# One encoder layer with a mixture of experts: first transfers, filler matmuls, norm rows and preloads rearranged

## The chip, the cores and the metric

The kernel runs on one core of one Trainium2 chip. The metric is the time of one execution on the device in microseconds; a kernel's time is the median of several executions, and lower is better. A core has TensorE (PE in the profile, its weight loads PEld), VectorE (DVE), ScalarE (ACT), GpSimd (POOL) and SyncE (SP); SP only issues transfers here, and all large loads go through its one queue. Transfers between the chip's memory (HBM) and the on-chip memory are carried out by 16 DMA engines. Matmul results land in PSUM, in banks of 128 x 512 floats.

## What is computed

One layer over 512 tokens of width 1024, in float32: three token mixers side by side (neighbourhood attention, grouped-query attention, attention into 256 memory tokens), gated and projected, a layer norm, and then a mixture of 16 experts of which each picks 64 tokens, with a second layer norm. Cut to its frame:

```python
mkv = jnp.einsum('bmd,df->bmf', mem, w_mem_kv[l])      # memory keys and values, the first work
...
merged = jnp.sum(gates * proj, axis=2)
mix = jnp.einsum('bsd,de->bse', merged, w_out[l])
x = layer_norm(DN_ALPHA * x + mix, ln1_g[l], ln1_b[l])
ffn = expert_choice_ffn(x, w_router[l], w_gate_up[l], w_down[l])
x = layer_norm(DN_ALPHA * x + ffn, ln2_g[l], ln2_b[l])

def expert_choice_ffn(x, w_router, w_gate_up, w_down):
    aff = softmax(x @ w_router)                        # 512 x 16
    gate, idx = top_k(aff per expert, 64)              # each expert picks 64 tokens
    h = x[idx] @ w_gate_up                             # 16 x 64 x 2048
    ye = (silu(hg) * hu) @ w_down                      # 16 x 64 x 1024
    return zeros.at[idx].add(ye * gate)
```

The expert weights are 16 x (8 MB + 4 MB), 192 MB of some 250 MB that the kernel moves.

## The kernel before

**Order.** The program is written with a manual schedule: each engine runs its instructions in the order in which the Python code issues them, and waits only for data and for buffers. Buffers come from pools by tag; a tag with two or three buffers is taken in turns, and a new tile in a buffer waits until the old one has been read. PSUM has the tags `mm` (3 banks), `S` (2), `T` (2) and `Y` (1), line 60.

**The start (lines 182 to 209, `g_mem`).** Dense products before the experts are done in two pieces for precision: `hi_lo` (line 84) makes a rounded copy of an operand on ScalarE (L85) and the remainder on VectorE (L86), and three matmuls are summed, hi x hi, hi x lo and lo x hi (`t_piece`, lines 244 to 249). The weights before the experts come as 74 units of 512 KB; `Stream` loads and splits them a little ahead. The first work needs the transposed memory rows `memr` (1 MB) and unit 0, so both are loaded in three pieces each, in turns (L197 memory, L198 unit), of 2, 2 and 4 of the 8 slices k of the contraction. Behind them on SP stand units 1 to 5, then the four quarters of x in turns with units 6 to 9. `k_item(h)` makes the memory keys of head h from unit h: 24 matmuls of 256 columns.

**The middle.** Attention, gates and branch projections run with TensorE as the busiest engine. At the end of it the output projection (`wo_part`, lines 992 to 999; `w_rest`, line 1018) is done in parts per 128-token tile m, with the layer norm's statistics, router logits and top-64 search of earlier tiles between its parts.

**The routing stretch (lines 1047 to 1118).** After the last part of tile 3, TensorE transposes pieces of x (`r_transpose`), forms logits (`r_logits`), transposes affinities (`r_back`); VectorE does the row scale, the softmax (`affinity`) and the rounds of the top-64 search (`rounds`); ScalarE and GpSimd write the normed rows as two half-precision pieces (`x1_norm`, lines 983 to 988). `keep_warm(n)` issues n filler matmuls, identity by identity, whose result in a bank `warm2` is never read. `thp` broadcasts the cut per expert, `cnp` counts positions.

**The experts.** `Ring` (line 731) streams the expert weights in 192 pieces of 1 MB through 22 buffers, most of which belong to earlier stages and come free as these end: the order is the list `RING`; the last are `Ma` and `Mb` (x and its norm), and `VS` (a triangle for `cnp`). `ring.done` issues the next load when a piece has been used. The order is gate and up 0 to 3 of an expert, the four down pieces of the one before, gate and up 4 to 7; at the end the eight pieces of expert 15, the down pieces of expert 14, then those of 15, which are cut by quarters of the output columns. Per expert e: `gate_up` (L1184), `act_h`, and in the next expert's loop `h_transpose` and `down` (L1217). Side work is stepped between: `gather` of the next four experts' tokens (in the loop of e = 3, 7, 11), `residual`, and `combine`, which adds a pair of experts' results into `ACC` (4 token tiles of 1024 columns).

**The last expert and the tail.** In the loop of e = 15 stand, between its two halves, `ln_row` (eight small matmuls that broadcast the second norm's gain to all partitions, copied to `g2` by ScalarE) and `rows_of_norm` (eight matmuls that make six rows `gb` of gain and bias for a low-rank product). Then `last_down` does expert 15's down product by quarters q of 256 columns: `product(q)` (L1333, and its split into hi and lo on ScalarE and VectorE), for q = 0, 1 `add(q)` (scatter into a bank, sum into `ACC` on VectorE, statistics, multiplication by the gain on GpSimd), for q = 2, 3 `preload(q)` (L1325: `ACC` copied into PSUM by an identity matmul) and `add_in_psum(q)` (scatter on top of it), then statistics from PSUM. After the statistics of all quarters: mean and scale per row, transposed to rows, `times_g_psum` for q = 2, 3, and `low_rank` and `diag` matmuls that finish the norm before the stores.

Of the kernel before, what the change touches and what calls it, by code (L numbers as in the profile page):

```python
# [18 lines left out]
P = 128  # L19
D = 1024  # L20
# [21 lines left out]
def layer_kernel(ctx: ExitStack, tc: tile.TileContext, xt, xn, memt, wu, bgate, rpb, gains, wrt,  # L42
# [139 lines left out]
    memh = R("A3", [P, KD, 256], "memh", F32R)  # L182
    meml = R("A4", [P, KD, 256], "meml", F32R)
    memr = R("A2", [P, KD, 256], "memr")
    raw0 = twin("raw")
    hi0 = hi_tile(0)
    lo0 = lo_tile(0)
# [21 lines left out]
    ws.hl[0] = (hi0, lo0)  # L209
# [55 lines left out]

    ST = {}

    def g_mem():
# [7 lines left out]
        def k_item(h):  # L276
# [3 lines left out]
            t_unit(acc[:, :256], u, memh, meml)  # L280
# [766 lines left out]
    warm2 = PB("T", "warm2")  # L1047

    def keep_warm(n):
        for _ in range(n):  # L1050
            nc.tensor.matmul(warm2[:, :P], ident, ident, start=True, stop=True)
# [38 lines left out]
    keep_warm(26)  # L1090
# [13 lines left out]
    nc.tensor.matmul(thp[:, :NEXP], ones_f[:NEXP], dg, start=True, stop=True)  # L1104
    msk = cp.tile([P, NT, 2, NEXP], F16, name="msk")
# [10 lines left out]
    keep_warm(3)  # L1116
# [81 lines left out]
    def h_transpose(e):  # L1198
        h = HT[e]
        tp = PB("mm", f"ht{e}", (P, 4, P))  # L1200
# [90 lines left out]
    def rows_of_norm():  # L1291
# [17 lines left out]
    def last_down(g2):  # L1309
# [8 lines left out]
        cols = [slice(q * 256, q * 256 + 256) for q in range(4)]  # L1318
        for mp in range(2):
            acc_of(2 * mp)  # L1320
        xq = {(q, mp): PB("ST"[mp], f"xq{q}{mp}", (P, 2, 256)) for q in (2, 3) for mp in range(2)}

        def preload(q):
            for mp in range(2):
                nc.tensor.matmul(xq[q, mp], ident, ACC[mp][:, :, cols[q]], start=True, stop=False)  # L1325
# [45 lines left out]
        def stats(q, m):  # L1371
            nc.vector.bn_stats(st[:, m, q], xq[q, m // 2][:, m % 2])
# [264 lines left out]
```

## Time and profile before

| | us |
|---|---|
| median of 3 runs (lowest, highest) | 989.99 (987.61, 991.37) |
| the profiled execution's own time | 987.18 |
| its span | 985.4 |
| TensorE busy | 957.7 (97%) |
| VectorE busy | 452.0 (46%) |
| ScalarE busy | 269.6 (27%) |
| GpSimd busy | 75.0 (8%) |

The DMA engines moved 251.59 MB, 255 GB/s over the span, and 425 to 427 GB/s in the slices of the expert stage. The mean granted clock of TensorE was 0.991 of full speed. The profile shows one execution; times in it are microseconds from the span's start unless marked ns. A timeline row gives start, duration, engine, line, operation, output and inputs, shapes, and in brackets how long the engine had been idle and what ended that. A row of a stretch ("windows") gives its length, then the busy time and the number of instructions of PE, PEld, DVE, ACT and POOL, the granted clock, the busy share of the DMA engines and GB/s. A row of SyncE's waits gives who waited for what, the sum, the number of times and the longest. A matmul of two float32 operands shows as two rows.

### The profile page before, as it was taken

To read this page: it belongs to the slowest core of one execution; us is meant where nothing else is said; L and a number is where in the kernel's file an instruction comes from. 1 tells how busy PE (TensorE), PEld (TensorE's weight loads), DVE (VectorE), ACT (ScalarE), POOL (GpSimd) and SP (SyncE) were. 2 spreads that over 40 slices of the span, in tenths; PEclk is the share of its full clock that TensorE was granted. 3 is DMA by queue.
4 is the path that set the end of the run, shared out by engine and by line. 5 is a ranking of instruction groups with operands and counts; after the bars stand their busy time and mean duration, and the time that the engine had idled before them with its cause. 6 is when DMAs were issued, how large, how long until landed. Compare 5 with 4: busy or idle time off the path is not lost.

```text
span 985.4 us, 13380 instructions
## 1 busy us (share of the span) xinstructions
PE 957.7 (97%) x5412; PEld 624.7 (63%) x5412; DVE 452.0 (46%) x855; ACT 269.6 (27%) x532; POOL 75.0 (8%) x82
## 2 busy tenths in 40 slices
PE   8999999999999999999999999999999999997998
PEld 7999877889888888887886334433343333432445
DVE  5437768665276566236463155331332223230327
ACT  4434344454354454323232010100010001100121
POOL 0002303000032231000021000000000000000002
PEclk8999999999999999999999999999999999999999
DMA  8322111111343322575729999999999999999982
GB/s 342 101 71 81 60 48 65 63 46 44 91 123 109 102 81 77 219 280 187 263 104 410 401 426 426 425 427 425 427 425 425 427 427 427 426 427 426 427 368 86
DMA packets 52605, 251.59 MB, mean 255 GB/s; under 512 B 14112, under 2 KB 14784, under 8 KB 28992
## 3 DMA queue, kind: packets, MB, share of 16 engines
q1 hardware_dynamic: 51968, 249.44, 63.2%
q10 hardware_dynamic: 576, 1.31, 0.3%
q8 instruction: 42, 0.69, 0.3%
q14 instruction: 19, 0.16, 0.0%
HBM read 247.84 MB, written 2.10 MB: 254 GB/s over the span
## 4 chain that ended last, share of the span: by engine, by line
PE 76%; DMA 12%; DVE 6%; ACT 2%; POOL 2%; issue 1%; SPq 0%; DVEq 0%; POOLq 0%; ACTq 0%
PE g L1184 9%; PE u L1184 8%; DMA gu<-in_wgu 8%; PE y L1217 8%; PE gate L247 4%; DMA dn<-in_wdn 4%; PE gate L248 4%; PE gate L249 4%; PE nqk L248 1%; PE nqk L247 1%; PE nqk L249 1%; PE gy L590 1%; PE pr L247 1%; PE ga L1149 1%; PE pr L248 1%
## 5 line engine op out<-in xcount | busy, mean ns | idle before, releaser
L1184 PE MATMUL g<-gu,xs 128*64 128x512 f32 x512 | 135.6, 608 | 3.7 <-DMA gu<-in_wgu 3.7
L1184 PE MATMUL u<-gu,xs 128*64 128x512 f32 x512 | 132.5, 596 | 0.0
L1217 PE MATMUL y<-dn,hT 128*64 128x512 f32 x480 | 106.4, 593 | 2.5 <-DMA dn<-in_wdn 2.4
L85 ACT CAST y<-y 64x512 fp32r<-64x512 f32 x30 | 17.4, 581 | 247.6 <-PE y L1217 217.7
L1184 PEld LDWEIGHTS u<-gu,xs 128*64 128x64 f32 x512 | 37.0, 138 | 73.7 <-issue 72.6
L86 DVE TENSOR_TENSOR y<-y,y 64x512 fp32r<-64x512 f32 x30 | 20.7, 689 | 136.6 <-ACT y L85 136.6
L1217 PEld LDWEIGHTS y<-dn,hT 128*64 128x64 f32 x480 | 34.0, 137 | 71.6 <-issue 63.8
L86 DVE TENSOR_TENSOR lo_twin<-raw_twin,whi 128x1024 fp32r<-128x1024 f32 (+2 forms) x46 | 55.2, 1199 | 51.7 <-ACT whi L85 51.5
L85 ACT CAST whi<-raw_twin 128x1024 fp32r<-128x1024 f32 (+2 forms) x67 | 68.7, 1026 | 17.7 <-PE wo L999 8.7
L1184 PEld LDWEIGHTS g<-gu,xs 128*64 128x64 f32 x512 | 31.4, 136 | 61.2 <-issue 45.1
L1288 DVE TENSOR_TENSOR acc<-acc,cb 128x512 f32<-128x512 f32 x56 | 35.5, 684 | 35.0 <-PE cb L1286 35.0
L86 DVE TENSOR_TENSOR wlo<-raw_twin,whi 128x1024 fp32r<-128x1024 f32 x21 | 27.4, 1305 | 36.9 <-ACT whi L85 36.8
L1205 DVE COPY hT<-ht 128x512 f32<-128x512 f32 x16 | 11.1, 691 | 61.3 <-PE ht L1202 61.3
L247 PE MATMUL gate<-xha,whi 128*128 128x512 f32 x96 | 38.9, 406 | 0.0
L1350 POOL TENSOR_TENSOR acc<-acc,ln2g 128x512 f32<-128x512 f32 x4 | 5.1, 1282 | 439.6 <-DVE l2s L1362 439.4
L248 PE MATMUL gate<-xla,whi 128*128 128x512 f32 x96 | 37.5, 390 | 0.0
L247 PE MATMUL gate<-xhb,whi 128*128 128x512 f32 x96 | 37.3, 389 | 0.0
L248 PE MATMUL gate<-xlb,whi 128*128 128x512 f32 x96 | 37.3, 389 | 0.0
L566 ACT ACTIVATE P_twin<-gs,nm 128x512 f32<-128x512 f32 x32 | 21.7, 684 | 52.3 <-DVE nm L565 52.3
L1194 ACT ACTIVATE tg<-g 128x512 f32<-128x512 f32 x16 | 9.6, 598 | 90.6 <-PE g L1184 90.6
L249 PE MATMUL gate<-xha,lo_twin 128*128 128x512 f32 x80 | 31.2, 390 | 0.0
L249 PE MATMUL gate<-xhb,lo_twin 128*128 128x512 f32 x80 | 31.1, 389 | 0.0
(423 smaller groups left out, 1958.1 us busy)
## 6 DMA issues: line engine op xcount, KB each, us to landing
gu<-in_wgu SPq DMA_DIRECT2D x123, 1024.0 KB
dn<-in_wdn SPq DMA_DIRECT2D x59, 1024.0 KB
raw_twin<-in_wu SPq DMA_DIRECT2D x65, 512.0 KB
gu<-in_wgu SPq DMA_DIRECT2D x10, 512.0 KB
dn<-in_wdn SPq DMA_DIRECT2D x10, 512.0 KB
raw<-in_wu SPq DMA_DIRECT2D x8, 512.0 KB
xr<-in_xt SPq DMA_DIRECT2D x4, 512.0 KB
x<-in_xn SPq DMA_DIRECT2D x2, 1024.0 KB
```

The costliest lines, as they stand in the source:

```text
L85: nc.scalar.copy(hi, src)
L86: nc.vector.tensor_tensor(lo, src, hi.bitcast(F32), op=ALU.subtract)
L247: nc.tensor.matmul(acc, w_h, rh[:, k], start=(k == 0), stop=False)
L248: nc.tensor.matmul(acc, w_h, rl[:, k], start=False, stop=False)
L249: nc.tensor.matmul(acc, w_l, rh[:, k], start=False, stop=(k == nk - 1))
L566: nc.scalar.activation(self.p[:, h], self.s[h], AF.Exp, bias=nm[:, h:h + 1], accum_out=self.sm[:, h:h + 1])
L590: nc.tensor.matmul(self.y[h * 64:h * 64 + 64, :P], ST["vg"][:, kc, kvh * 64:kvh * 64 + 64], self.pt[:, h, kc], start=(kc == 0), stop=(kc = ...
L1149: nc.tensor.matmul(g, XH[:, m, c], oh[:, m], start=(m == 0), stop=False)
L1184: nc.tensor.matmul(GU[e][b][hf * 64:hf * 64 + 64], xs, w[b][:, hf * 512:hf * 512 + 512], start=(k == 0), stop=(k == KD - 1))
L1205: nc.vector.tensor_copy(t, tp)
L1217: nc.tensor.matmul(y[o * 64:o * 64 + 64], hT[:, c, hf * 64:hf * 64 + 64], w[j][:, o * 512:(o + 1) * 512], start=(k == 0 and j == 0), stop= ...
L1288: nc.vector.tensor_tensor(a, a, cb, op=ALU.add)
```

## The change

Four things change.

1. The host packs the memory rows and unit 0 into one input `first0` (128 x 4 x 768: two k slices of memory rows, 512, and of unit 0, 256), which replaces `memt`. It is loaded in four transfers, each split whole; `first_unit` does head 0's keys part by part, with a part's two hi x hi products first. `memh` and `meml` become a view (`Mem`) of the parts.
2. In the routing stretch `keep_warm` takes a bank of its own at each call, and the counts become 3 (new), 11 (from 5), 28 (from 26), 1 (new) and 4 (from 3).
3. `ln_row` for the second norm and the rest of `rows_of_norm` move from the loop of e = 15 to that of e = 12 (the 13th expert), stepped between its first four gate and up pieces; buffer `A5` (the half-precision rows) is free from there on.
4. `preload(2)` and `preload(3)` move from `last_down` into the loop of e = 15, behind gate and up pieces 1 and 5. In the tail the four products write into halves of two banks, `yq`; product and split are apart; the first bank of `add` is a bank `spare`, the second one `cbl` for both quarters; the last split stands behind the statistics of quarter 2 on VectorE; the gain of quarter 2 is multiplied before the statistics of quarter 3; the fillers are 22 (from 18) and 3 (from 2); the banks of the last matmuls differ.

```diff
-    parts = ((0, 2), (2, 4), (4, 8))
-    for a, b in parts:
-        nc.sync.dma_start(memr[:, a:b], memt[:, a:b])
-        nc.sync.dma_start(raw0[:, a * P:b * P], wu[0, :, a * P:b * P])
+    for i in range(4):
+        nc.sync.dma_start(fr[i // 2][:, i % 2], first0[:, i])
...
-    for a, b in parts:
-        hi_lo(memh[:, a:b], meml[:, a:b], memr[:, a:b])
-        c = slice(a * P, b * P)
-        hi_lo(hi0[:, c], lo0[:, c], raw0[:, c])
+    for i in range(4):
+        hi_lo(fh[i // 2][:, i % 2], fl[i // 2][:, i % 2], fr[i // 2][:, i % 2])
...
+    def first_unit(acc):
+        for i in range(4):
+            ks = (2 * i, 2 * i + 1)
+            for k in ks:
+                nc.tensor.matmul(acc, first_part(fh, k, 512, P), memh[:, k], start=(k == 0), stop=False)
+            for k in ks:
+                nc.tensor.matmul(acc, first_part(fh, k, 512, P), meml[:, k], start=False, stop=False)
+                nc.tensor.matmul(acc, first_part(fl, k, 512, P), memh[:, k], start=False, stop=(k == KD - 1))
...
-    warm2 = PB("T", "warm2")
-
     def keep_warm(n):
+        warm2 = PB("T", "warm2")
         for _ in range(n):
             nc.tensor.matmul(warm2[:, :P], ident, ident, start=True, stop=True)
...
     w_rest(3, 256, 256, 2, {1: then(lambda: r_transpose(3, 4, 2), third), 2: lambda: r_logits(3, 4, 2)})
+    keep_warm(3)
     r_transpose(3, 6, 2)
     r_back(2)
     r_logits(3, 6, 2)
-    keep_warm(5)
+    keep_warm(11)
     all_of(row_scale((3,), 3))
     norm_cols((3,))
     all_of(affinity((3,)))
     r_back(3)
     x1_norm(2)
     x1_norm(3)
-    keep_warm(26)
+    keep_warm(28)
...
+            if e == 12:
+                g2 = R("A5", [P, D], "ln2g")
+                side = rows_of_norm(g2)
...
-            gate_up(e, range(4))
+            gate_up(e, (0, 1))
+            x2 = preload(2, "ST")
+            gate_up(e, (2, 3))
             h_transpose(e - 1)
             slots_T(e // 2)
-            g2 = R("A5", [P, D], "ln2g")
-            for h in range(2):
-                nc.scalar.copy(g2[:, h * 512:(h + 1) * 512], ln_row(2, h, f"g2{h}"))
-            all_of(rows_of_norm())
-            gate_up(e, range(4, KD))
+            gate_up(e, (4, 5))
+            x3 = preload(3, ("mm", "mm"))
+            gate_up(e, (6, 7))
+            spare = PB("mm", "spare")
...
         product(0)
-        preload(2)
+        split(0)
         product(1)
+        split(1)
         add(0)
         product(2)
-        preload(3)
+        split(2)
         add(1)
         product(3)
         add_in_psum(2)
         for m in range(NT):
             stats(2, m)
+        split(3)
         add_in_psum(3)
-        keep_warm(18)
+        for mp in range(2):
+            times_g_psum(2, mp)
+        keep_warm(22)
...
-        for q in (2, 3):
-            for mp in range(2):
-                times_g_psum(q, mp)
+        for mp in range(2):
+            times_g_psum(3, mp)
```

More of the change, by code (lines that the diff above doesn't have):

```diff
@@ L279, in k_item @@
             acc = PB("mm", f"mk{h}")
-            t_unit(acc[:, :256], u, memh, meml)
+            if h == 0:
+                first_unit(acc[:, :256])
+            else:
+                t_unit(acc[:, :256], u, memh, meml)
             if h >= 2:
@@ L1289, in combine, with rows_of_norm @@
                 yield
-    def rows_of_norm():
+    def rows_of_norm(g2):
+        for h in range(2):
+            bc = ln_row(2, h, f"g2{h}")
+            yield
+            nc.scalar.copy(g2[:, h * 512:(h + 1) * 512], bc)
         sl, cc = (small([6, 1], n, bufs=1) for n in ("gb_s", "gb_c"))
```

94 lines of the change are left out of this document (50 added, 44 removed).

## The prediction

> **What bounds the kernel now.** I read the page first (busy shares, clock, DMA by slice), then SyncE's own waits, then stretches of the span, then the timeline of the four places that the change touches.
>
> ```profile
> span 985.4 us, 13380 instructions
> ...
> DMA  8322111111343322575729999999999999999982
> ```
> ```profile
> SPq L139 <- DVE lo_twin L86: 212.5, 33, 17.9
> ...
> SPq L763 <- PE woc L998: 24.4, 1, 24.4
> ```
> ```profile
> 504.00:508.00 4.00, 4.00 (x36) 4.00 (x35) 3.73 (x23) 2.79 (x4) 0.00 (x0) 1.00 0.00 0
> ...
> 516.00:520.00 4.00, 3.27 (x17) 3.00 (x16) 2.44 (x13) 2.88 (x6) 0.14 (x1) 0.50 1.00 418
> ```
> ```profile
> sum 480.00, PE 469.53 PEld 401.51 DVE 278.84 ACT 201.30 POOL 59.05; mean PE 9.78 PEld 8.36 DVE 5.81 ACT 4.19 POOL 1.23
> ```
>
> There are three regimes. From 0 to 480 us TensorE is busy 469.53 of 480: it is the bound, and the weight loads wait for VectorE (212.5 us), not the reverse. Just before 508 us the DMA engines stand idle, because the next expert weight waits 24.4 us for the last output-projection matmuls (L998) to free its buffer. From about 511 us on, the DMA row shows 9 in every slice until the weights are in: the expert weights (1 MB each, some 427 GB/s, so an estimated 2.46 us each) are the bound, and TensorE, the faster of the two, catches up with them late. That regime ends with the first product of the last down projection, which waits for its transfer until 953.92 (row in part 3). What follows, 31.5 us, is the tail. So the time is: when the projection frees the buffers, plus the stream, plus the tail. Something saved before 508 us counts in full; something saved on TensorE between 530 and 950 us counts for nothing.
>
> **Part 1, four equal first transfers.** Six loads of 128 to 512 KB (memory rows and the first weight unit, L197 and L198) become four of 384 KB, each split by one cast and one subtraction, and `first_unit` does both high-high matmuls of a part before it asks for the low halves. The first hi/lo buffers and one `hi` rotation go away.
>
> ```profile
> 6.00:8.00 2.00, 1.80 (x9) 1.21 (x9) 1.03 (x2) 0.89 (x2) 0.00 (x0) 1.00 0.76 256
> 8.00:10.00 2.00, 0.43 (x4) 0.23 (x2) 0.00 (x0) 0.16 (x1) 0.00 (x0) 0.78 1.01 407
> ...
> 14.00:16.00 2.00, 2.00 (x12) 2.00 (x11) 1.65 (x3) 0.90 (x2) 0.00 (x0) 0.52 1.03 422
> ```
> ```profile
> 4.31 0.62 ACT L85 CAST memh<-memr 128x512 fp32r<-128x512 f32 x1 [2.30 <-DMA memr<-in_memt]
> ...
> 4.96 0.69 DVE L86 TENSOR_TENSOR meml<-memr,memh 128x512 fp32r<-128x512 f32 x1 [4.96 <-ACT memh L85]
> ...
> 9.84 1.05 ACT L85 CAST memh<-memr 128x1024 fp32r<-128x1024 f32 x1 [2.95 <-DMA memr<-in_memt]
> ...
> 10.79 0.62 ACT L85 CAST whi<-raw_twin 128x512 fp32r<-128x512 f32 x1
> 10.92 1.23 DVE L86 TENSOR_TENSOR meml<-memr,memh 128x1024 fp32r<-128x1024 f32 x1 [3.28 <-ACT memh L85]
> ...
> 11.46 0.58 PE L247 MATMUL mk<-memh,whi 128*128 128x256 f32 x1 [3.03 <-ACT whi L85]
> ...
> 11.70 1.05 ACT L85 CAST whi<-raw_twin 128x1024 fp32r<-128x1024 f32 x1 [0.29 <-DMA raw_twin<-in_wu]
> 12.06 1.94 DVE L86 TENSOR_TENSOR lo_twin<-raw_twin,whi 128x512 fp32r<-128x512 f32 x2
> ...
> 14.68 0.41 PE L248 MATMUL mk<-meml,whi 128*128 128x256 f32 x1
> ...
> 14.89 0.41 PE L249 MATMUL mk<-memh,lo_twin 128*128 128x256 f32 x1
> ...
> 18.10 0.28 PE L248 MATMUL mk<-meml,whi 128*128 128x256 f32 x1
> ...
> 18.22 0.28 PE L249 MATMUL mk<-memh,lo_twin 128*128 128x256 f32 x1
> ```
>
> TensorE starves for 3.03 us until 11.46, finishes unit 0 at half clock (0.52 over 14 to 16: full only from about 15.9), and issues the last matmul of unit 1 at 18.22. After: the same 1.57 MB. If nothing arrives sooner than now, the last part is there at about 10.4 (the last two pieces are cast from 9.84 and 10.79); at the 407 GB/s of 8 to 10 us throughout it would be there at 2 + 1.57/0.407 = 5.9. I take 8.5, nearer the slow end, because shares of 0.76 at full queues show engines waiting rather than working. A 768-wide cast lies midway between 0.62 and 1.05, 0.84; the subtraction midway between 0.69 and 1.23, 0.96. Unit 0 is then done near 11 instead of 15.1. It isn't the next limit: unit 1 needs its low half, ready at 12.06 + 1.94 = 14.0 now, an estimated 12.3 with loads and casts 1.7 us earlier. From the low half on, 22 matmuls remain, 0.21 us apart at half clock to 15.9 (14.68 to 14.89), 0.12 after (18.10 to 18.22). Ready at 14.0, that is 9 then 13, end 17.5 (0.9 sooner than 18.34); ready at 12.3, 17 then 5, end 16.5 (1.8 sooner). With a full clock from 12.5 it would be 14.9 (3.4 sooner). I take 1.3 us; bounds 0.5, if a 384 KB part comes a little later than a 256 KB one, and 3.4. A loss is excluded: unit 1's load is issued two loads earlier than now. Later loads land well ahead of their use, so the lead stays until the buffers come free at 509: worth -1.3 at the end.
>
> The Trainium skill ("DMA: Bandwidth & Descriptors", Specifications) gives 512 bytes as the smallest transfer at line rate; by that, runs of 1 and 2 KB were no worse than the new 3 KB, the parts land as now, and the sum's first term would be the -0.9 of the slow end. The trace doesn't settle it: 256 GB/s at 6 to 8 us came with both small and 4 KB runs.
>
> **Part 2, dummies in the routing stretch.** Three more before `r_transpose(3, 6, 2)`, 11 for 5 ahead of `r_back(3)`, 28 for 26, one behind `thp`, 4 for 3.
>
> ```profile
> 512.68 0.44 PE L911 MATMUL x1t<-ident,x 128*128 128x128 f32 x2 [0.97 <-DVE x L928]
> ...
> 514.04 2.28 PE L1051 MATMUL warm<-ident 128*128 128x128 f32 x10
> ...
> 517.06 0.37 PE L971 MATMUL ap<-ident,rt 128*16 128x128 f32 x1 [0.73 <-DVE rt L966]
> ...
> 517.22 7.82 PE L1051 MATMUL warm<-ident 128*128 128x128 f32 x52
> ```
> ```profile
> 969.61 4.18 PE L1384 MATMUL warm_l<-ident 128*128 128x128 f32 x36
> ```
>
> A dummy is two rows: 4.18/18 = 0.232 us at full clock, 2.28/5 = 0.456 at half. The three fill 0.70 of the 0.97 us hole, so the clock probably stays up. Then 11 x 0.232 = 2.55 end at 516.6, before the affinities are there (517.06 less the hand-over): nothing waits, and the few small transposes save some 0.3 us. At half clock 11 x 0.456 = 5.0 end at 519.05, and behind them stand `r_back(3)`, then on ScalarE `x1_norm(2)` and `(3)`, which free the weight buffers Ma and Mb: 2.0 us late. I take -0.3; bounds -0.8 and +2.1.
>
> By the Trainium skill ("TensorE: Matmul & The Clock Gate", HAM oscillation) only idle gaps above some 3.4 us throttle, so dummies would buy nothing here and the term would be 0. The trace disagrees: the longest hole here is 0.97 us and the clock was 0.50.
>
> **Part 3, the norm's rows in the 13th expert, preloads in the 16th.**
>
> ```profile
> 886.00:896.00 10.00, 7.80 (x34) 2.03 (x32) 1.98 (x3) 1.02 (x2) 0.00 (x0) 1.00 1.01 425
> 896.00:906.00 10.00, 8.45 (x38) 2.63 (x40) 0.69 (x1) 0.00 (x0) 0.00 (x0) 1.00 1.01 424
> 906.00:916.00 10.00, 7.69 (x34) 2.01 (x34) 1.38 (x2) 1.16 (x2) 0.00 (x0) 1.00 1.02 428
> ```
> ```profile
> 933.42 2.05 PE L1253 MATMUL g<-lnr,ident 32*128 32x128 f32 x16
> ```
> ```profile
> 935.39 1.91 PE L1302 MATMUL gbr<-lnr,gb_sel 32*6 32x128 f32 x16
> ```
> ```profile
> 953.92 1.97 PE L1333 MATMUL yq<-dn,hT 128*64 128x128 f32 x32 [0.30 <-DMA dn<-in_wdn]
> ...
> 955.82 1.98 PE L1325 MATMUL xq<-acc,ident 128*128 128x512 f32 x4
> ...
> 960.93 0.69 DVE L1360 TENSOR_TENSOR acc<-acc,cbl 128x512 f32<-128x512 f32 x1
> ...
> 961.65 0.75 DVE L1362 BATCH_NORM_STATS2 l2s<-acc 128x6 f32<-128x256 f32 x2
> ...
> 969.01 1.76 DVE L1372 BATCH_NORM_STATS2 l2s<-xq 128x6 f32<-128x256 f32 x5
> ...
> 972.55 0.26 DVE L1401 BATCH_NORM_AGGREGATE l2mv<-l2s 128x2 f32<-128x24 f32 x1
> ...
> 974.47 2.48 DVE L1375 TENSOR_TENSOR acc<-xq,ln2g 128x512 f32<-128x512 f32 x4
> ...
> 974.71 0.60 PE L1414 MATMUL rowT<-ident,ch 128*6 128x128 f32 x4 [0.91 <-DVE ch L1410]
> ```
>
> The rows cost TensorE 2.05 + 1.91 = 3.96 us, and four copies on ScalarE and six small operations on VectorE go with them. In expert 12 they delay TensorE, but between 886 and 916 it stood idle 2.20 + 1.55 + 2.31 = 6.06 us for weights: the delay is taken out of that wait, 2.1 left over. Without that cover they would cost 3.96. In expert 15 two preloads (2 x 1.92 by issue, the 1.98 row) take the place of the 3.96: nothing gained or lost before 953.92, where TensorE waits for the transfer. Term 0.
>
> **Part 4, the tail.** The preloads no longer stand between the products, 3.84 us of TensorE. It isn't gained whole. The four transfers land at an estimated 953.8, 956.2, 958.7, 961.1 (2.46 apart, the first from the wait), so the second product starts at 956.4, the first `add` at 958.3, the third product at 959.5, `add(1)` at 961.4, the fourth at 962.5. VectorE becomes the bound: the split of quarter 1 ends 959.55; `add(0)` takes 0.69 + 0.75 + 0.67 + 0.75 = 2.86, to 962.4; split 0.6; `add(1)` to 965.9; four statistics from PSUM, 1.45, to 967.3; the last split 0.6; then two multiplications by the gain that used to come later, 2 x 0.62, to 969.2; statistics and aggregates of the last quarter as now (970.4, behind four of the five in the row at 969.01, to 972.81: 2.4) to 971.6. That is 1.2 us sooner. But 22 dummies now start when the last low-half matmul ends, 968.7, and end at 968.7 + 5.1 = 973.8, where the transposes could go at 971.6 + 1.9 = 973.5: 0.3 lost. One more dummy behind them costs about 0.1. The low-rank and diagonal matmuls behind it stay TensorE's, so the two multiplications taken off VectorE there bring nothing. I take -0.8; bounds -1.2 and, since TensorE now idles about 1.9 us from 966.1 and the clock may drop, 22 dummies with 3 us at half: +0.6.
>
> **Sum.** -1.3 - 0.3 + 0 - 0.8 = -2.4 on the profiled execution's own 987.18 us (span 985.4 and 1.8 around it): 984.8. That execution lies 2.8 below the median 989.99 of the runs shown, so the median should be 987.6.
>
> **Rivals.** (a) The lead is bigger: full clock from 12.5 us and none lost to dummies, -3.4 - 0.3 - 1.2 = -4.9: 985.1. For it: 24 matmuls that come sooner may lift the activity of that stretch; against: TensorE still idles between the parts, as in the row of 8 to 10 us, where 0.43 of 2 busy left it at half. (b) The lead doesn't arrive: some wait between 20 and 509 us is set by a clock of its own, the first term is 0, -1.1: 988.9. For: 10.5 us of idle in 480; against: VectorE and GpSimd chains that start from TensorE's own results move with it. (c) On the other side, one mechanism: dummies issued in order at half clock, in front of work that is ready. It decides from the point where a clock window opens on the hole at 511 us or the one at 966. Price +2.1 in routing and +0.6 in the tail against -1.3: +1.4, 991.4, slower than before. For: the clock was at 0.50 exactly where the 11 now stand; against: the three dummies in the hole. (d) The rows in expert 12 aren't absorbed: 3.96 - 2.4, 991.5; against it, 6.06 us of idle. I give it with (c).
>
> **How the numbers follow.** Forecast 0.50, (a) 0.23, (b) 0.12, (c) and (d) 0.15. Half a per cent, 4.95 us, is about what a measurement of this kernel can tell from no change (its three runs span 3.8). Below 985.04: of (a) 0.17, of the forecast 0.10, by scatter: 0.27. Above 994.94: of (c) and (d) 0.06, of (b) 0.01: 0.07. The rest, 0.66. The likeliest's own range is 985.2 to 990.0; with (a) and (c) and the scatter of medians 983.4 to 991.9.
>
> **What would show it.** Right: unit 1's last matmul near 17, idle DMA ending near 508, the clock at 1.0 through 512 to 521, idle TensorE of some 2 us left between 886 and 916, the last aggregate 18 us after the first last-down product (now 972.81 - 953.92 = 18.9). Wrong: `r_back(3)` waiting behind dummies; the first product waiting for TensorE instead of a transfer; the projection's end unmoved; a larger gain if the stream itself runs faster than 427 GB/s.

## The result and the profile after

| | before | after |
|---|---|---|
| median of 6 runs, us | 990.03 (987.61 to 991.37) | 982.10 (981.07 to 984.66) |
| ratio of the runs, 95% interval | | 0.9928 (0.9910 to 0.9946) |
| the profiled execution's own time | 987.18 | 982.14 |
| its span | 985.4 | 980.3 |

The change makes the kernel 0.7% faster, 7.9 us by the medians and 5.0 by the two profiled executions. The forecast was 987.6, with 983.4 as the lower end of its range.

First the head of the page after, with the granted clock and the DMA row in 40 slices:

```profile
span 980.3 us, 13446 instructions
...
PEclk9999999999999999999999999999999999999998
DMA  9322111211333322675639999999999999999992
```

The three regimes are the same; the idle DMA ends earlier in its slices. SyncE's own waits say the same, with the 24.4 us for the projection unchanged, so the stream starts as before when the projection frees its buffers:

```profile
SPq L781 <- PE woc L1016: 24.4, 1, 24.4
```

The first load after that wait was issued at 509.52 us before and at 505.74 after. The span divides at four moments that both traces show (first load after the hole, first last-down product, last aggregate, end):

| stretch | before | after | difference | predicted |
|---|---|---|---|---|
| start to first load | 509.52 | 505.74 | -3.78 | -1.3 |
| first load to first last-down product | 444.40 | 442.92 | -1.48 | -0.3 |
| product to end of last aggregate | 18.9 | 16.9 | -2.0 | -1.2 |
| last aggregate to end | 12.58 | 14.75 | +2.2 | +0.4 |

These are two single executions, and two of the four rows don't carry over to others, as is seen below: the second is scatter, and the last goes with where the clock falls.

The start, in the stretches of the changed kernel that were shown of before (columns as there: TensorE's busy time second, granted clock, DMA share and GB/s last):

```profile
6.00:8.00 2.00, 1.98 (x13) 1.60 (x13) 1.86 (x2) 0.83 (x1) 0.00 (x0) 1.00 0.98 363
8.00:10.00 2.00, 1.20 (x6) 0.78 (x6) 0.89 (x1) 1.38 (x2) 0.00 (x0) 1.00 1.03 410
...
14.00:16.00 2.00, 2.00 (x19) 2.00 (x19) 1.18 (x3) 1.35 (x2) 0.00 (x0) 1.00 1.03 422
...
516.00:520.00 4.00, 3.79 (x34) 3.60 (x33) 3.42 (x15) 2.56 (x4) 3.75 (x4) 1.00 1.01 428
886.00:896.00 10.00, 9.89 (x48) 3.07 (x44) 1.81 (x3) 0.86 (x2) 0.00 (x0) 1.00 1.01 428
896.00:906.00 10.00, 8.57 (x40) 2.51 (x36) 0.69 (x1) 0.00 (x0) 0.00 (x0) 1.00 1.02 424
906.00:916.00 10.00, 8.08 (x34) 2.84 (x36) 2.94 (x5) 1.16 (x2) 0.00 (x0) 1.00 1.01 425
```

Two things differ at 6 to 16 us: 363 GB/s for 256, and a clock of 1.00 for 0.78 and 0.52. At 516 the clock is full (0.50 before). From 886 to 916 TensorE idles 0.11 + 1.43 + 1.92 = 3.5 us, 6.06 before. The timeline of the same start shows one of the two short holes that are left in unit 0 (0.44 and 0.49 us, in place of 3.03), the wait for unit 1's low half, and unit 1's last matmul:

```profile
8.25 0.83 ACT L85 CAST firsth<-first 128x768 fp32r<-128x768 f32 x1 [1.34 <-DMA first<-in_first]
...
9.13 0.51 PE L276 MATMUL mk<-firsth 128*128 128x256 f32 x2 [0.44 <-ACT firsth L85]
...
11.82 0.39 PE L255 MATMUL mk<-firsth,lo_twin 128*128 128x256 f32 x1 [0.71 <-DVE lo_twin L86]
...
14.44 0.28 PE L255 MATMUL mk<-firsth,lo_twin 128*128 128x256 f32 x1
```

14.44 for 18.22 is 3.78 us, and exactly 3.78 stand at the first load: the lead goes through 490 us whole. The other profiles bear that out: from unit 1's last matmul to the first load it is 491.2 to 491.3 us in 13 of the 19, whatever the start, and about 1.5 more in four with a half-clock stretch near 100 us. In the remaining two, fillers stand in the way. Now the tail, products, statistics, fillers, last aggregate and the last matmuls:

```profile
948.66 1.97 PE L1361 MATMUL yqS<-dn,hT 128*64 128x128 f32 x32 [0.29 <-DMA dn<-in_wdn]
...
950.42 1.94 PE L1361 MATMUL yqT<-dn,hT 128*64 128x128 f32 x32
...
953.50 1.97 PE L1361 MATMUL yqS<-dn,hT 128*64 128x128 f32 x32
...
956.79 1.97 PE L1361 MATMUL yqT<-dn,hT 128*64 128x128 f32 x32 [0.17 <-DMA dn<-in_wdn]
...
962.51 5.08 PE L1408 MATMUL spare<-ident 128*128 128x128 f32 x44
...
965.32 0.26 DVE L1429 BATCH_NORM_AGGREGATE l2mv<-l2s 128x2 f32<-128x24 f32 x1
...
967.47 0.60 PE L1442 MATMUL rowT<-ident,ch 128*6 128x128 f32 x4
...
969.62 1.12 PE L1460 MATMUL lr<-acc,dgr 128*128 128x512 f32 x2
...
971.58 1.80 PE L1460 MATMUL lr<-acc,dgr 128*128 128x512 f32 x2
...
974.03 2.08 PE L1460 MATMUL lr<-acc,dgr 128*128 128x512 f32 x2
```

```profile
930.00:940.00 10.00, 10.00 (x48) 3.49 (x44) 0.69 (x1) 0.63 (x2) 0.00 (x0) 1.00 1.02 428
...
970.00:975.00 5.00, 5.00 (x9) 1.56 (x8) 2.82 (x5) 1.17 (x2) 0.00 (x0) 0.69 0.82 315
975.00:980.00 5.00, 1.83 (x3) 0.28 (x1) 0.00 (x0) 0.58 (x1) 0.00 (x0) 0.50 0.27 105
```

The last aggregate comes 7.2 us sooner than before. But a pair of matmuls of the same form takes 1.12 us at 969.6 and 2.08 at 974: the clock fell to half at 971.89, though TensorE was busy without a hole in the 3.41 us ahead of it:

```profile
968.48:971.89 3.41, 3.41 (x12) 1.61 (x11) 2.54 (x5) 1.67 (x5) 0.00 (x0) 1.00 0.27 104
```

That is where 2.2 us go again in this execution. It is not a price of the new tail. With the tail of before the same happens: in the profile of part 2 alone, whose tail is the old one, the last aggregate to the end takes 14.85 us for 12.58, and in that of the eight small first transfers with fillers 14.89. The matmuls in the first of these:

```profile
976.58 1.13 PE L1434 MATMUL lr<-acc,dgr 128*128 128x512 f32 x2
...
981.04 2.08 PE L1434 MATMUL lr<-acc,dgr 128*128 128x512 f32 x2
```

So the profiled execution of the kernel before had a full clock at its end, and that of the changed kernel had not; the 5.0 us between the two understate the change by that much.

The 1.48 in the second row is the transfers'. A transfer lands in 16 shares, and the trace records the time of each. By these records, the first share of the first last-down transfer came 3.81 us sooner, as the lead says, and the last share 5.26 sooner:

```
                                      before            after
three transfers ahead (first..last)   941.00..945.05    937.19..941.19
first last-down transfer              948.37..953.78    944.56..948.52
last transfer                         955.74..961.09    951.95..956.75
16 KB of instruction code (0.9 us)    946.45            954.69
```

The last share trailed the first by some 4 us in both streams. It trailed by 5.4 to 5.5 for the last seven transfers before (from 943.44..948.92 on), and by 4.8 for the very last one after. A 16 KB transfer of instruction code lies near each of the two places, but others (922.75 before, 934.40 after) brought no growth, so a cause is not shown. The 1.48 itself is no gain of the change. From the first load of the stream to the landing of the first last-down transfer it is 442.3 to 444.3 us in the 19 profiles of all kernels. The longest is that of before, 444.26; it is 443.3 and 443.4 in two runs whose stream starts at the same time as before (part 2 alone, the rows alone).

### The profile page after: what moved, and what is told of

It reads as the page before. It is cut to its first block, busy times and chain, and to the rows that moved or that the text cites. A ratio compares the mean times of both kernels' runs of the same rounds, so it can differ in the third digit from the quotient of the medians.

```text
span 980.3 us, 13446 instructions
## 1 busy us (share of the span) xinstructions
PE 957.3 (98%) x5448; PEld 624.2 (64%) x5448; DVE 451.6 (46%) x852; ACT 269.2 (27%) x531; POOL 75.2 (8%) x82
## 4 chain that ended last, share of the span: by engine, by line
PE 79%; DMA 8%; DVE 6%; ACT 2%; POOL 2%; issue 1%; SPq 0%; DVEq 0%; POOLq 0%; ACTq 0%
PE g L1203 10%; PE u L1203 9%; PE y L1236 8%; DMA gu<-in_wgu 6%; PE gate L253 4%; PE gate L254 4%; PE gate L255 4%; DMA dn<-in_wdn 2%; PE cb L1304 2%; PE ga L1168 1%; PE nqk L253 1%; PE nqk L255 1%; PE nqk L254 1%; PE gy L608 1%; PE pr L253 1%
## 5 line engine op out<-in xcount | busy, mean ns | idle before, releaser
L86 DVE TENSOR_TENSOR lo_twin<-raw_twin,whi 128x1024 fp32r<-128x1024 f32 x43 | 53.8, 1252 | 51.9 <-ACT whi L85 51.8
L85 ACT CAST whi<-raw_twin 128x1024 fp32r<-128x1024 f32 x64 | 67.2, 1051 | 17.5 <-PE wo L1017 8.7
```

What stands on the lines that cost most here:

```text
L85: nc.scalar.copy(hi, src)
L86: nc.vector.tensor_tensor(lo, src, hi.bitcast(F32), op=ALU.subtract)
```

## The experiments

All times are differences of medians to the kernel before, run beside it, with the interval of the ratio.

**One part at a time.** Part 1 alone is the diff's `first0`, `first_unit` and `Mem`; nothing else.

> The kernel before with part 1 alone (four first transfers, first_unit). Theory: in the changed kernel's trace the first weight load after the hole was issued at 505.74 us against 509.52 before, and unit 1's last matmul stands at 14.44 against 18.22, the same 3.78; so part 1 alone gives the whole of it: last matmul of unit 1 at 14.4 to 14.6, clock 1.00 over 0 to 20, first load of the stream at 505.7 to 505.9, and the time 3.8 below the kernel before (3.3 to 4.3). Rival: a part of the 3.78 comes from elsewhere or is lost again without the dummies of part 2: the load still at 505.7 but the time only 2 below.

Measured: -3.74 us, 0.9956 (0.9939 to 0.9974), so between 2.6 and 6.0 us; that it meets the 3.78 of the trace so closely is luck. Unit 1's last matmul at 14.41. The first load stood at 507.19 in this execution, not 505.7. Its stretches show why, and something else:

```profile
96.00:100.00 4.00, 2.19 (x14) 1.53 (x14) 3.38 (x9) 2.56 (x8) 0.00 (x0) 1.00 0.00 0
100.00:104.00 4.00, 4.00 (x23) 4.00 (x23) 3.37 (x11) 1.53 (x6) 0.00 (x0) 0.57 0.00 0
...
930.00:940.00 10.00, 10.00 (x50) 5.04 (x49) 3.47 (x9) 2.91 (x5) 0.00 (x0) 0.66 1.00 424
```

A hole of 1.81 us at 97 is followed by 3.41 us of half clock, which cost some 1.4; the changed kernel had the same hole at 97 and no such stretch. And with the norm rows still in the last expert the clock was at 0.66 from 930 to 940: the first last-down product started at 951.77, 2.0 us after its transfer (949.80 by the records of its shares). The lead is 3.8 us; part of it is lost again in this execution, at 100 us and where TensorE is late. Nor does every execution of the new start keep its clock: in two of the eight profiles that have it without fillers (the rows put back, and 128 rows, both below) the clock fell to half at 12 us, and unit 1's last matmul stood at 15.45 and 15.55.

Part 2 alone:

```diff
+    keep_warm(3)
     r_transpose(3, 6, 2)
...
-    keep_warm(5)
+    keep_warm(11)
...
-    keep_warm(26)
+    keep_warm(28)
```

> The kernel before with part 2 alone (the counts of the fillers in the routing stretch). Theory: the stream of weights starts with the projection's end, which part 2 does not touch, so the time stays within 0.5 of the kernel before, though the last cnp matmul comes 0.4 to 1.5 earlier after the stream's first load than its 17.2 us before (526.75 - 509.52) and the clock stays at 1.00 from 512 to 521. Rival: the half clock in the routing stretch costs the stream something at Ma, Mb and VS, and the dummies give 1.5 to 2 us. Rival on the other side: the dummies themselves fall into a half-clock window: 1 to 2 us slower.

Measured: +0.73, 1.0008 (0.9993 to 1.0023): no gain. The clock was at 1.00 from 512 to 521, and the stream did not care. The same part taken out of the changed kernel:

> The changed kernel with the routing stretch's fillers as before (part 2 undone). Theory: the stream starts before the routing and its loads are the bound behind it, so nothing moves: within 0.7 of the changed kernel, whether or not a half window falls on 512 to 528. Rival: with the stream 3.8 earlier the routing, not the transfers, decides when TensorE is through at 954, and the fillers are worth 1 to 2 us.

Measured: -5.87, 0.9938 (0.9923 to 0.9954), the changed kernel beside its variants -5.94. Part 2 is worth nothing that can be measured at either end. One half window did fall on 521 to 525 in that profile, without effect on the first product.

Parts 3 and 4 alone, and the rows of part 3 alone (`rows_of_norm` in the loop of e = 12, the rest as before):

> The kernel before with parts 3 and 4 alone (norm rows in the 13th expert, preloads in the 16th, the new tail). Theory: from the first product of the last down projection to the last aggregate 16.9 us as in the changed kernel (18.9 before), first product at 953.9 less up to 1.4; from the last aggregate to the end 12.6 if the clock stays full there, 14.7 if it falls to half as in the changed kernel. So 2.0 faster with a full clock at the end, 0 with a half one. Rival: the rows in the 13th expert delay the weights, and the first product comes 1 to 4 us later.

> The kernel before with part 3's first half alone: the norm rows in the 13th expert, preloads and tail as before. Theory: the clock stays at 1.00 from 930 to 945 (0.88 before), idle TensorE between 886 and 916 falls from 6.1 to about 2, and the first product, which in three of the variants so far stood 1.0 to 2.4 us behind its transfer, now starts with it: 1 to 2 us faster than before. Rival, as predicted: 0, since the first product waits for its transfer anyhow. Rival on the other side: the rows are not absorbed at 886 to 916: 2 to 4 slower.

Measured: parts 3 and 4 -3.16, 0.9967 (0.9953 to 0.9981); the rows alone -0.48, 0.9996 (0.9982 to 1.0011), less than the 1 to 2 of its theory. With both parts the first load stood at 508.35 (1.2 sooner than before with the same start, because the half clock lay at 11.13 to 14.54 in place of 9.10 to 15.93), the first product at 951.83, the last aggregate ended at 968.75 and the span at 981.39: 443.5, 16.9 and 12.6. So the tail gives its 2.0 whole where the clock holds at the end: 16.9 us in all eleven profiles with the new tail, 18.8 to 18.9 in all seven with the old one. The 0.9 in the stretch ahead of it is within the scatter of the stream (442.3 to 444.3).

**The whole, and the rows put back.**

> The changed kernel itself, to stand beside its variants on one chip. Theory: the parts add: part 1 alone took 3.74 off the median and parts 3 and 4 alone 3.16, part 2 nothing, so 6.5 to 7.5 below the kernel before. Rival: they share a gain (both bring the last products to the transfers), and the whole is less than the sum, 5 or less below.

Measured: -5.94, 0.9938 (0.9918 to 0.9958). The sum of the parts is -3.74 + 0.73 - 3.16 = -6.2: they add, as far as intervals of some 1.5 us to either side can tell. The profile again had the clock at half from 972.

```diff
-            if e == 12:
-                g2 = R("A5", [P, D], "ln2g")
-                side = rows_of_norm(g2)
...
             slots_T(e // 2)
+            g2 = R("A5", [P, D], "ln2g")
+            all_of(rows_of_norm(g2))
```

> The changed kernel with the norm rows back in the loop of the last expert (between its fourth and fifth weight piece), everything else as changed. Theory: TensorE is busy without a hole from 916 to 950 us and reaches the first last-down product hardly 0.3 us before its transfer, so the 3.96 us of the rows, and half a clock window that their narrow matmuls bring (1.7 for each of 3.4 us), go straight to the end: clock below 1 between 925 and 940, first product 3.5 to 5.5 us later than in the changed kernel and waiting for TensorE, time 3 to 5.5 us above it. Rival, the prediction's own step: the transfer decides and the rows cost nothing at that place: the same time.

Measured: -3.51, 0.9974 (0.9958 to 0.9990), 2.4 above the changed kernel, less than the 3 to 5.5 expected; the clock did not fall between 925 and 940 in this profile, so the half-window part of the expectation was not seen. The first product by the timeline:

```profile
955.68 1.92 PE L1361 MATMUL yqS<-dn,hT 128*64 128x128 f32 x32
```

No wait stands behind it, and its transfer was there at 952.16: TensorE was 3.5 us late. Moving the rows is worth 0.5 alone (an interval across 0) and 2.4 together with the preloads: it makes the room that the preloads take.

**Part 1: clock or data?** First the clock alone: the kernel before with 12 fillers in unit 0's hole.

```diff
                 for k in range(KD):
+                    if k == 4:
+                        for _ in range(12):
+                            nc.tensor.matmul(warm[:, :P], ident, ident, start=True, stop=True)
```

> The kernel before with its six first transfers, and 12 filler matmuls (12 x 0.232 = 2.8 us) in the hole of unit 0 at 8.4 to 11.5 us, ahead of its fifth k slice: the clock alone, without earlier data. Theory: the gain of part 1 has two halves: data 2.2 us earlier (the second unit's load landed at 9.43 against 11.67) and a clock that stays full. With the clock alone unit 0 ends near 14.1, and unit 1's 24 matmuls at 0.12 put its last at 16.9: 1.3 sooner than 18.22, and the time 1.3 lower. Rival 1: the clock is all of it: last matmul near 14.5, time 3.8 lower. Rival 2: the clock is nothing of it, or the fillers are themselves at half clock: last matmul at 18.2 or later, time the same or up to 2 higher.

Measured: -1.77, 0.9976 (0.9962 to 0.9989); last matmul of unit 1 at 16.36, first load at 507.61. Then the data without the packing, and without and with fillers:

```diff
-    parts = ((0, 2), (2, 4), (4, 8))
+    parts = ((0, 2), (2, 4), (4, 6), (6, 8))
```

> The kernel before with its first transfers cut into four equal pairs in place of three (memory rows in runs of 2 KB, unit 0 in runs of 1 KB; eight transfers): equal parts without the packing. Before, the 1 MB of the last pair came at 250 GB/s (6.3 to 10.42 us), the packed parts of 384 KB at 390 GB/s (4.10, 5.05, 6.05, then 8.22). Theory A: what counts is that a part's two halves come together in equal order: the last pair there at 8.2 to 9, unit 1's last matmul near 15 to 16, 2 to 3 us faster than before. Theory B: what counts is the number of pieces that the DMA engines handle (1024 runs of 1 and 2 KB here, 768 of 1 to 4 KB before, 512 of 3 KB packed): the last pair at 10.4 or later, gain 0 to 1 (from the hole in unit 0 being cut in two), or a loss.

> The kernel before with eight small first transfers (as in the run of that name) and fillers in its holes (2 ahead of the fifth slice of unit 0, 3 and 3 in unit 1's first slice). Theory: earlier data pays only with a full clock: unit 1's load lands at 10.55 (11.67 before, 9.43 packed), its low half is there at 12.9, and 22 matmuls at 0.12 put the last one at 15.5 to 15.7: 2.6 sooner than before, time 2 to 2.8 lower; the last 1.1 of part 1's 3.8 is then the packing, by four issues of SyncE (0.47 each) fewer ahead of unit 1's load. Rival: the clock falls all the same, or small transfers are slower for what comes behind: 0 to 1 lower, as without fillers.

Measured: -0.38, 0.9994 (0.9979 to 1.0009) without fillers, -2.85, 0.9973 (0.9957 to 0.9989) with them; unit 1's last matmul at 17.05 and 15.53. The stretch of 14 to 16 us without and then with them:

```profile
14.00:16.00 2.00, 2.00 (x11) 2.00 (x11) 1.54 (x3) 0.15 (x1) 0.00 (x0) 0.50 1.03 420
```

```profile
14.00:16.00 2.00, 2.00 (x19) 2.00 (x18) 1.68 (x4) 0.41 (x2) 0.00 (x0) 1.00 1.03 420
```

The expectation has a slip: the last pair of before is 768 KB, not 1 MB, so it came at 191 GB/s over the 4.12 us. The eight transfers' last piece landed at 8.79 (10.42 before, 8.22 packed) with runs of 1 and 2 KB, so theory B falls: the number of runs was not the limit. Theory A falls too as it stood, because early data under half clock gained 1.2 us at unit 1's end and nothing measurable in time. Together: clock 1.86 (18.22 to 16.36), equal parts 0.83 (to 15.53), and the packing 1.1 (to 14.41), with which unit 1's load landed at 9.41 for 10.53. These steps come from single profiles and are good to some half a microsecond: with the first transfers of before, unit 1's load landed at 10.76 to 11.68 in five profiles, the run of the clock alone (11.18) among them. That the packing's share is due to its four issues fewer on SyncE is argued, not tried by itself.

**The end.** 128 rows in the low-rank product in place of 6 (`gb` and `rows` widened, zeros against ones in the other 122):

> The changed kernel with the low-rank product of the tail over 128 rows in place of 6 (ones against zeros in the other 122; same columns, same number of matmuls, same result). Theory: the clock falls at the end (972 to 980 us, after a stretch with TensorE busy 1.00) because matmuls with 6 of 128 rows count as little work; with 128 rows it stays full to about 978, the last aggregate to the end takes 12.6 in place of 14.7 us, and the time is 1 to 2 us below the changed kernel. Rival: rows don't count, the clock falls in the same way, and the time is the same.

Measured: -8.38, 0.9918 (0.9896 to 0.9940), 2.4 below the changed kernel. In its profile something else was late, seen in the timeline:

```profile
965.30 6.26 PE L1409 MATMUL spare<-ident 128*128 128x128 f32 x44
...
971.40 0.60 PE L1443 MATMUL rowT<-ident,ch 128*6 128x128 f32 x4
```

The hole ahead of the last scatter brought half clock at 964.38, the 22 fillers took 6.26 us for 5.08, and the transposed rows, ready 1.9 us after the last aggregate (967.97), went 3.4 after it. So 6 of the fillers go into that hole, alone and with the 128 rows:

```diff
         for n in range(2):
+            if q == 3 and n == 1:
+                keep_warm(6)
...
-        keep_warm(22)
+        keep_warm(16)
```

> The changed kernel with 6 of its 22 fillers ahead of the last low-half scatter, and the low-rank product over 6 rows as changed. Two prices were seen: fillers at half clock ahead of the transposed rows (3.4 us from the last aggregate to them in place of 1.9, in two profiles), and the last matmuls at half clock (14.7 us from the last aggregate to the end in place of 12.6, in the profiles with 6 rows where a clock window opened 2.8 to 2.9 us after the last aggregate). Theory: the moved fillers mend the first alone, and the low-rank product's narrow matmuls still bring the second: clock 0.994 to 0.998, 981.5 to 983, at most 1.5 below the changed kernel. Rival: the hole ahead of the scatter was the cause of both, the time is 979.6 as with both edits.

> The changed kernel with the end alone mended: low-rank product over 128 rows, 6 of the 22 fillers ahead of the last low-half scatter; no fillers at the start. Theory: the end's half window is what was given back: last aggregate to end 11.9 to 12.1 and the time 2 to 2.5 below the changed kernel's 983.0, with the start's windows (0 to 2.6 us) still in the spread. Rival: with the end's clock full something else ends last, and less than 1 is gained.

Measured: moved fillers alone -6.46, 0.9940 (0.9923 to 0.9956); both -9.43, 0.9910 (0.9895 to 0.9926). The last matmuls with both:

```profile
969.93 1.02 PE L1464 MATMUL lr<-acc,dgr 128*128 128x512 f32 x2
...
971.49 1.02 PE L1464 MATMUL lr<-acc,dgr 128*128 128x512 f32 x2
...
972.58 1.02 PE L1464 MATMUL lr<-acc,dgr 128*128 128x512 f32 x2
```

1.02 for 1.12 to 2.08, and 11.9 us from the last aggregate to the end for 14.75. Widening the rows is the larger part: 3.0 us by medians between the two runs, 2.4 between the changed kernel and the run with 128 rows alone, each known to 2 or 3 us only. Part of it has nothing to do with the clock. At full clock, too, the stretch takes 11.90 us with 128 rows and 12.54 to 12.64 with 6 (the profile with the fillers moved alone had a full clock to its end): 0.6 to 0.7 less. The weight loads (PEld) show where. They stand idle 0.76 us ahead of a load of 6 rows and 0.24 ahead of one of 128, here at full clock, first with the fillers moved alone, then with both:

```profile
973.65 0.18 PEld L1458 LDWEIGHTS lr<-gb,rows 6*128 6x128 f32 x1 [0.76 <-issue]
```

```profile
973.01 0.19 PEld L1460 LDWEIGHTS lr<-gb,rows 128*128 128x128 f32 x1 [0.24 <-issue]
```

The rest, up to 2.2 us, is the half clock, and that the 6 rows bring it is not shown by the profiles. In the traces the clock changes only at steps of 3.41 us, a grid of windows. With 6 rows it fell at the end of a window that opened 2.8 to 2.9 us after the last aggregate (five profiles), and stayed full through the last products where none opened then (nine). In none of the five profiles with 128 rows did a window open there (1.3, 2.6, 3.2, 3.2 and 3.4 us). For the rows speak the mean clocks of the executions: 0.994 to 0.997 in five of six with the fillers moved alone, 0.997 to 1.000 in all five with 128 rows as well.

**Holes filled from the start too.** Fillers in unit 0 (2 and 2), unit 1 (3) and, meant for the hole at 97 us, 6 in a memory-attention unit:

> The changed kernel with the low-rank product over 128 rows, fillers in the holes of the start (2 and 2 in the last part of unit 0, 3 in unit 1), 6 in the hole at 97 to 99 us, and 6 of the tail's 22 moved into the hole ahead of the last quarter's low-half scatter. Theory: what is left between executions of the changed kernel (979.7 to 983.7) is the place of the clock's half windows; with every hole filled the clock stays at 1.00 to within 4 us of the end, and the time is 979 to 980.5 in nearly every execution, 2 to 3 below the changed kernel. Rival: fillers delay work that is ready, or a window falls all the same: 982 or more, spread as before.

> The changed kernel with the fillers of the first 105 us alone. Theory: first load of the stream at 505.5 to 505.9 in each execution (507.2 and 508.4 were seen in variants with half windows near 12 and 101 us), no half window before 900; the end still at half clock from 972: 981.5 to 982.5, about 0.5 to 1 below the changed kernel. Rival: 7 plus 6 fillers are in the way: first load at 506.5 or later.

Measured: -7.44, 0.9927 (0.9913 to 0.9942) and -5.83, 0.9946 (0.9930 to 0.9962): less than the end alone gives (-9.43), and nothing from the start's fillers. The six stood in the first memory unit, at 64 us, where TensorE has no hole to fill: first load at 507.07 in the one, 1.33 behind the changed kernel's, about 6 x 0.232 = 1.39. In the other the hole at 97 stayed and half clock followed it. Put into the seventh unit, which has the hole, and then with one multiplication moved:

```diff
-        for mp in range(2):
-            times_g_psum(2, mp)
+        times_g_psum(2, 0)
...
+        times_g_psum(2, 1)
         for mp in range(2):
             times_g_psum(3, mp)
```

> The run with the clock held, with the 6 fillers in the unit that has the hole at 97 to 98.8 us (the seventh memory unit in place of the first). Theory: the first load of the stream at 505.6 to 505.9 in place of 507.07, no half window before the last 4 us, last aggregate to end 11.9, time 979 to 980 (9 to 10 below the kernel before, 3 below the changed kernel). Rival: the six cost as much there: 981.4 again.

> The same with the multiplication of quarter 2's second half by the gain behind the statistics of quarter 3 on VectorE (0.62 us off the way to the last aggregate). Theory: VectorE is the bound of the tail after the last transfer, so the last aggregate comes 0.5 to 0.6 sooner after the fourth product, and the time is 0.3 to 0.6 lower. Rival: the multiplication is late next, in front of the last matmuls, and nothing or 0.3 is lost.

Measured: -9.61, 0.9911 (0.9895 to 0.9926), first load at 505.71; with the multiplication later -10.28, 0.9903 (0.9887 to 0.9919), the last aggregate 8.4 us after the fourth product's start for 9.1. So the fillers of the start, even in the right holes, add nothing measurable to the end alone (-9.61 for -9.43). The later multiplication shows in the trace as the 0.65 that it takes off VectorE's way; by medians the step is smaller than the intervals. This last kernel, 978.77 us (978.13 to 978.95 in 5 runs), is the fastest; the 17 runs of the kernel before spread over 5 us in the same set.

## Why the prediction was wrong, point by point

The forecast moves the median by -2.4 us. Measured are -7.9 (-8.9 to -5.3 by the interval) and -5.9 in the repeat (-8.1 to -4.2). By the runs of the parts, two terms of the sum were too small, by some 2.4 us each: part 1, -3.7 where -1.3 was taken, and parts 3 and 4, -3.2 (-4.6 to -1.9) where -0.8 was taken; part 2, +0.7 for -0.3, is nothing. The 2.8 from the profiled execution to the median did no harm to the difference, but it was no constant of the measurement. The executions of the kernel before differ by their clock, 0.985 to 0.995 on the mean (0.985 to 0.989 in those above 990 us); the profiled one had 0.991, and a full clock behind its last aggregate.

1. **Part 1, "I take 1.3 us".** This is the first step that failed. The mechanism was right, but the term measured 3.78 in the trace and 3.74 alone, above even the upper bound of 3.4. It rested on "half clock to 15.9", which took the clock of before as given at a time of day, although the edit removes the 3.03 us hole ahead of it. With the clock full, worth up to 1.9 by the run of the clock alone, the data too came earlier than the 1.7 estimated: unit 1's load by 2.24. Rival (a) had this, at 0.23; the row of 8 to 10 us that was held against it belonged to the hole (the clock was full in it until 9.10 and half behind). That nothing of the lead is lost before 509 was right.
2. **Part 2, -0.3.** Nothing, as near as can be measured. The clock did hold at 512 to 521, and the routing chain's last `cnp` moved by 0.5 beyond the lead, but the weights behind it are the bound. Rival (c) in that place was wrong.
3. **Part 3, 0.** Right for the rows alone (0.5, interval across 0), and the idle time absorbed them. "Nothing gained or lost before 953.92" was right only for that execution: TensorE and the transfer were nearly level there. Between 916 and 950 TensorE is busy without a hole, so it is the rows' clock and the preloads' room that decide whether the product waits for a transfer: it was 1.0 to 2.7 us behind its transfer in five variants with the rows in the last expert and half clock between 933 and 942. Of the seven profiles with the rows there, in one block, six show such a stretch; the twelve with the rows in the 13th expert, stepped between wide products, show none there and none at 886 to 916. The row of the clock there (0.88 over 930 to 940) was not weighed:

```profile
930.00:940.00 10.00, 10.00 (x62) 5.38 (x60) 3.39 (x9) 2.91 (x5) 0.00 (x0) 0.88 1.01 426
```

4. **Part 4, -0.8.** This is the second step that failed: 2.0 to the last aggregate where 1.2 was given. VectorE did become the bound, as the run with one multiplication later shows. But the second product started 1.76 after the first, not some 2.5, because quarter 1 comes as two loads of 512 KB and can begin on the first (landed at 949.80, the second at 951.04); that is 0.7 of the 0.8. The +0.4 for fillers behind it did not come: the transposed rows went 1.88 us after the last aggregate, as before, and in the profile of parts 3 and 4, with a full clock, it is 12.64 us from there to the end for 12.58. The +2.2 between the two profiles in its place is the half clock of the low-rank products, not in the hole at 966 that was named; the old tail has it as well, so it is no cost of the edit. The 2.0 of the trace lies inside the interval of what parts 3 and 4 measured (1.9 to 4.6); whether there is more stays open.
5. **Rivals.** (a) came nearest, 985.1, in mechanism and sign, and still 3.0 above the measured median. (b), no lead, and (d), rows not absorbed, did not occur. (c) occurred in its tail half, in two variants (1.6 us of late transposes: 128 rows alone, and part 2 undone), not in the routing.

## What to carry to other kernels

Cost the clock as a consequence of the edit, not as a property of a time: whoever removes a hole can remove the half clock behind it, and narrow matmuls that stood in one block behind half clock brought none when they were stepped between wide ones. Compare two profiles only where both, or neither, have such a stretch. A step that waits for a transfer by a few tenths of a microsecond is level with the other engine, and work taken off that engine there is worth something as soon as anything else gets faster. A filler is free only inside a hole of that very instance; six of them six loop iterations too early cost 1.3 us.

## What the runs showed of the hardware that was not expected

- Half-clock stretches last 3.41 or 6.83 us (9.10 to 15.93, 937.52 to 940.94 before; those at the end run on to it), on a grid that lies differently in each execution. The same hole of 1.81 us stands in 17 profiles, somewhere in 96 to 103 us. In eight it lay within one window of the grid, and five of these were followed by half clock (part 1 alone is one); in nine it lay across two windows, and none was (the changed kernel is one). The Trainium skill ("TensorE: Matmul & The Clock Gate", Part 1: The HAM clock gate) says that the activity window is free-running and 3413 ns long; the traces agree. Its rule that only gaps above some 3.4 us throttle ("HAM oscillation") doesn't hold here: 1.81 us was enough in those five profiles.
- Busy is not the same as active. The clock fell at 971.89 behind a window with TensorE busy 3.41 of 3.41 us, with products of 6 rows among them, and at 937.52 before behind one with busy 3.41 of 3.41, with the narrow matmuls of the norm's rows. Nor does the busy share alone tell it elsewhere: 2.54 of 3.41 us busy (a window of before) was followed by half clock, 1.73 of 3.41 (a window of the changed kernel) was not:

```profile
5.69:9.10 3.41, 2.54 (x12) 1.62 (x11) 1.32 (x3) 0.93 (x2) 0.00 (x0) 1.00 0.86 299
```

```profile
118.56:121.97 3.41, 1.73 (x10) 1.19 (x10) 0.00 (x0) 0.14 (x1) 2.52 (x2) 1.00 0.35 137
```

That the few rows are the reason at the end is argued from the medians and mean clocks above, not shown by a profile.
- The 16 shares of a weight transfer land over 3.0 to 5.5 us in the last transfers of the stream. This spread grew by 1.4 us before, by 0.9 after and by 0.5 in the profile of part 1, each time near a 16 KB transfer of instruction code. Such transfers lie there in the other 16 profiles too, and in these it changed by 0.2 at most over the last nine transfers, so that they are the cause is not shown.
